# The tensor_tensor work of GpSimd moves to VectorE in a hybrid streaming-encoder block on one core

## The chip, the cores and the metric

The kernel runs on one core of a Trainium2 chip. Its time is the device time of one execution in microseconds (us). TensorE multiplies matrices into PSUM, VectorE and ScalarE work element by element on SBUF and PSUM, GpSimd does so on SBUF only, and SyncE issues the transfers between HBM and SBUF.

## The reference

One layer on a sequence of 2048 tokens with 1024 channels, all in float32. A token mixer and a channel mixer follow each other, each between two RMS norms, with a residual:

```
mix = token_mixer(rms_norm(x, pre_mix_g));       h = x + rms_norm(mix, post_mix_g)
ffn = channel_mixer(rms_norm(h, pre_ffn_g));     out = h + rms_norm(ffn, post_ffn_g)

token_mixer:   p = xn @ w_in
               group A: C * causal_conv3(B * hA)            512 channels
               group B: RWKV-7 mixing, 8 heads x 64, in chunks of 64 frames, then a group norm
               concat(A, B) @ w_out
channel_mixer: f = causal_conv3(hn @ w_up) + b              2 x 2816 channels
               (gelu(gate) * up) @ w_down
```

## The kernel before

Tensors lie channels by tokens, 128 channels on the partitions. The 2048 tokens are worked in four blocks of 512. Each float32 matrix product is made of three products of rounded halves: an operand is split into a high half (a ScalarE copy to the rounded type) and a low half (a subtraction, `split`, lines 484 to 486), and high x high, high x low and low x high are added in PSUM.

There are two plans, each with its own tiles. The first holds the token mixer: for each block the input projection (27 column groups of 128, eight weight tiles each, loaded four at a time by `gemm`, line 490), the RWKV mixing of two pairs of heads twice (features, scores, a triangular inverse by 31 steps of two VectorE instructions, a chain over eight chunks), the short convolution (`short_conv`, line 1148), then the output projection and the residual of the block ahead. The second plan holds the channel mixer: the up-projection of blocks 0 and 1 together (`up(0)`), two down-projections, the up-projection of blocks 2 and 3 (`up(1)`), two down-projections. The last output projection runs into `up(0)`, and two residuals are put beside its weight columns 8 and 14 (of 22).

What GpSimd does, apart from memsets at the start:

- In the first block `gemm` makes the low halves of the weights and keeps them in HBM; the later blocks load them from there. Low halves of the second four tiles of each column group (`keep and k0`) are made on GpSimd: 26 instructions.
- The first block's input norm is applied late, to products instead of the operand (`late` is its factor, broadcast). In `short_conv` two of these multiplies per column group are on GpSimd: 8 instructions.
- The up-projection multiplies two by two blocks of matrices with seven products instead of eight. The sums of weights that this wants are made in `up(0)` by `summed` (line 1342) and kept in HBM for `up(1)`. Of four sums per weight column, s1 (`wu0s`) and s3 (`wu2s`) are on GpSimd, s2 and s4 (both `wu1s`) on VectorE: 2 x 22 instructions on each.
- `finish` (line 1500) ends a down-projection: the norm's factor per token is spread over the partitions by a small product into PSUM (`over_partitions`, line 544; `fn_ps`), ScalarE copies it to SBUF (`fn_rb`), each of eight parts `fo` is multiplied by it and the residual `ho` is added, and the sum is stored. GpSimd multiplies parts 0 to 2 and adds parts 0 and 1, VectorE does the rest, reading the factor from PSUM. `ho` has two buffers, except in the last block, whose residuals are all held and whose tokens are finished in two halves of 256. `fo` lies in the eight buffers where the last operands of the next up-projection go.

The order on each engine is not that of the code. Every instruction is recorded with the instructions that it depends on, a rank and a modelled cost; `schedule` (line 364) lays them out as a list, the lowest rank first among those that are ready, `latest` (line 314) makes new ranks from how late each may start, and the best of 16 rounds is emitted. `cost` (line 264) gives a VectorE tensor_tensor of n columns 66 + 1.045 n ns and a GpSimd one 148 + 2.1 n ns: 601 and 1223 ns for 512 columns. Since all instructions are emitted at one place, the profile gives line 431 for nearly all; they are told apart by the tiles that they write and read.

Of the kernel before, what the change touches and what calls it, by code (L numbers as in the profile page):

```python
# [15 lines left out]
ALU = mybir.AluOpType  # L16
# [5 lines left out]
TB = 512  # L22
# [429 lines left out]
def tile_block(ctx: ExitStack, tc: tile.TileContext, x_tok, x_t, w_in, w_out, w_up, w_down,  # L452
# [3 lines left out]
    dve = nc.vector  # L456
    pool_e = nc.gpsimd
# [4 lines left out]
    o1 = plan.pool(ctx, "o1", 1)  # L462
# [27 lines left out]
    def gemm(ps, src, nk, xs, name, keep=None, early=False):  # L490

        old = plan.rank
        for k0 in range(0, nk, 4):
            n = min(4, nk - k0)
            plan.rank = R_PREP if early else R_WEIGHT
            raw = wst.tile([128, 4, 128], F32, tag="wraw", name=f"{name}_r{k0}", bufs=WB[0])
            nc.sync.dma_start(out=raw[:, 0:n, :], in_=src[:, k0:k0 + n, :])
            hi = wst.tile([128, 4, 128], F32R, tag="whi", name=f"{name}_h{k0}", bufs=WB[1])  # L500
            lo = wst.tile([128, 4, 128], F32R, tag="wlo", name=f"{name}_l{k0}", bufs=WB[1])
            if (keep, k0) in lower:
                act(hi, raw, AF.Copy)
                nc.sync.dma_start(out=lo.bitcast(F32), in_=lower[keep, k0])
            else:
                split(raw[:, 0:n, :], hi[:, 0:n, :], lo[:, 0:n, :],
                      pool_e if keep and k0 else dve)
                if keep:
                    lower[keep, k0] = dram.tile([128, 4, 128], F32, name=f"{keep}_l{k0}")
                    nc.sync.dma_start(out=lower[keep, k0], in_=lo.bitcast(F32))  # L510
            plan.rank = R_GEMM
            for k in range(n):
                wh, wl = hi[:, k, :], lo[:, k, :]
                ah, al = xs[k0 + k]
                nc.tensor.matmul(ps, wh, ah, start=(k0 + k == 0), stop=False)
                nc.tensor.matmul(ps, wh, al, start=False, stop=False)
                nc.tensor.matmul(ps, wl, ah, start=False, stop=(k0 + k == nk - 1))
        plan.rank = old
# [22 lines left out]
                          op0=ALU.mult, op1=ALU.add)  # L541
        rsqrt(o1, ms, [128, n], name, out=out)

    def over_partitions(y, name, pool, tag, bufs=1, both=False, n=4):

        dg = o1.tile([128, 4, 128], F32, tag="sq", name=f"{name}_dg")
        ps = psN.tile([128, TB], F32, tag="g", name=f"{name}_ps")
        for s in range(n):
            dve.tensor_scalar(out=dg[:, s, :], in0=ident, scalar1=y[:, s:s + 1], scalar2=None,
                              op0=ALU.mult)  # L550
        with plan.together():
            for s in range(n):
                nc.tensor.matmul(ps[:, s * 128:(s + 1) * 128], ones, dg[:, s, :],
                                 start=True, stop=True)
        rb = pool.tile([128, TB], F32, tag=tag, name=f"{name}_rb", bufs=bufs)[:, 0:n * 128]
        ps = ps[:, 0:n * 128]
        act(rb, ps, AF.Copy)
        return (rb, ps) if both else rb

    def token_sums(accs, name, n=4):  # L560

# [115 lines left out]
    with ExitStack() as mctx:  # L677
# [75 lines left out]
        with ExitStack() as ictx:  # L753
# [394 lines left out]
            def short_conv(b, j):  # L1148

                plan.rank = R_EVAC  # L1150
                nm = f"{b}_{j}"
                u = m1.tile([128, TB + 2], F32, tag="u", name=f"u{nm}", bufs=1)
                act(u[:, 0:2], ucar[:, j, :], AF.Copy)
                ps = proj(15 + 3 * j, f"ch{nm}")
                if late is None:
                    act(u[:, 2:TB + 2], ps, AF.Copy)
                else:
                    dve.tensor_tensor(out=u[:, 2:TB + 2], in0=ps, in1=late, op=ALU.mult)
                ps = proj(16 + 3 * j, f"cb{nm}")
                dve.tensor_tensor(out=u[:, 2:TB + 2], in0=ps, in1=u[:, 2:TB + 2], op=ALU.mult)  # L1160
                if late is not None:
                    pool_e.tensor_tensor(out=u[:, 2:TB + 2], in0=u[:, 2:TB + 2], in1=late,
                                         op=ALU.mult)
                act(ucar[:, j, :], u[:, TB:TB + 2], AF.Copy)
                cv = m1.tile([128, TB], F32, tag="cv", name=f"cv{nm}", bufs=1)
                act(cv, u[:, 2:TB + 2], AF.Copy, scale=v_("conv_a", 8 + j))
                dve.scalar_tensor_tensor(out=cv, in0=u[:, 1:TB + 1], scalar=v_("conv_a", 4 + j),
                                         in1=cv, op0=ALU.mult, op1=ALU.add)
                dve.scalar_tensor_tensor(out=cv, in0=u[:, 0:TB], scalar=v_("conv_a", j),
                                         in1=cv, op0=ALU.mult, op1=ALU.add)  # L1170
                ps = proj(17 + 3 * j, f"cc{nm}")
                dve.tensor_tensor(out=cv, in0=ps, in1=cv, op=ALU.mult)
                if late is not None:
                    pool_e.tensor_tensor(out=cv, in0=cv, in1=late, op=ALU.mult)
                nc.sync.dma_start(out=y_d[b][:, j, :], in_=cv)

            def first_operand():
# [111 lines left out]
    with ExitStack() as fctx:  # L1289
# [35 lines left out]
        def up_weights(s, i):  # L1325


            nm = f"{s}_{i}"

            def load(src, name, base=RAW, n=6):  # L1330
                raw = next_slot(base, n, f"wu{name}{nm}", F32, (128, 4, 128))
                nc.sync.dma_start(out=raw, in_=src)
                return raw

            def parts(raw, name):
                plan.rank = R_WEIGHT
                hi = wst.tile([128, 4, 128], F32R, tag="whi", name=f"wu{name}{nm}_h", bufs=WB[1])
                lo = wst.tile([128, 4, 128], F32R, tag="wlo", name=f"wu{name}{nm}_l", bufs=WB[1])
                split(raw, hi, lo, dve)
                return hi, lo  # L1340

            def summed(a, b, op, j, engine, o=None):
                plan.rank = R_WEIGHT
                if o is None:
                    o = next_slot(SUM, 2, f"wu{j}s{nm}", F32, (128, 4, 128))
                engine.tensor_tensor(out=o, in0=a, in1=b, op=op)
                nc.sync.dma_start(out=s_d[i][:, j, :, :], in_=o)
                return o

            plan.rank = R_WEIGHT  # L1350
            ga, gb, ua, ub = (w_up[j][:, k:k + 4, :] for j in (i, NF + i) for k in (0, 4))
            if s == 0:
                a11, a12, a21, a22 = (load(x, n) for x, n in ((ga, "a11"), (gb, "a12"),
                                                              (ua, "a21"), (ub, "a22")))
                yield parts(a11, "a11")
                s1 = summed(a21, a22, ALU.add, 0, pool_e)
                yield parts(s1, "s1")
                s2 = summed(s1, a11, ALU.subtract, 1, dve)
                yield parts(s2, "s2")
                yield parts(a12, "a12")  # L1360
                s3 = summed(a11, a21, ALU.subtract, 2, pool_e)
                yield parts(s3, "s3")
                s4 = summed(a12, s2, ALU.subtract, 3, dve, s2)
                yield parts(s4, "s4")
                yield parts(a22, "a22")
            else:
                for src, n in ((ga, "a11"), (s_d[i][:, 0, :, :], "s1"), (s_d[i][:, 1, :, :], "s2"),
                               (gb, "a12"), (s_d[i][:, 2, :, :], "s3"), (s_d[i][:, 3, :, :], "s4"),
                               (ub, "a22")):
                    plan.rank = R_WEIGHT  # L1370
                    yield parts(load(src, n, RAW, 8), n)
# [101 lines left out]
        def down_block(b, beside=None):  # L1473
# [26 lines left out]
            def finish(t, accs):  # L1500
# [3 lines left out]
                n = (t.stop - t.start) // 128  # L1504
                rf = f1.tile([128, 4], F32, tag="rf", name=f"rf{nm}")[:, 0:n]
                inv_rms(token_sums(accs, nm, n), nm, rf, n)
                rb, rps = over_partitions(rf, nm, o1, "nrb", both=True, n=n)
                for d in range(KT):
                    if last:
                        hk = held[d][:, t]  # L1510
                    else:
                        hk = f1.tile([128, TB], F32, tag="ho", name=f"ho{b}_{d}", bufs=2)
                        nc.sync.dma_start(out=hk, in_=h_d[b][:, d, :])
                    fd = fo[d][:, t]
                    if d < 3:
                        pool_e.tensor_tensor(out=fd, in0=fd, in1=rb, op=ALU.mult)
                    else:
                        dve.tensor_tensor(out=fd, in0=fd, in1=rps, op=ALU.mult)
                    (pool_e if d < 2 else dve).tensor_tensor(out=hk, in0=fd, in1=hk, op=ALU.add)
                    nc.sync.dma_start(out=out_t[:, b, d, t], in_=hk)  # L1520

            tokens = slice(0, TB)
# [123 lines left out]
```

## Time and profile before

| | |
|---|---|
| time, median of 3 runs | 2590.94 us (2590.84 to 2595.94) |
| profiled execution | 2591.45 us |
| its span, first to last instruction | 2589.7 us |
| TensorE busy | 2479.0 us (96%) |
| VectorE busy | 2025.0 us (78%), 4159 instructions |
| ScalarE busy | 1476.6 us (57%) |
| GpSimd busy | 152.8 us (6%), 116 instructions |
| mean granted TensorE clock | 0.986 of full speed |
| HBM traffic | 166 GB/s over the span |

Busy time is the time in which at least one instruction of the engine runs; two instructions that overlap count once. TensorE's share is an average over stages with different limits, so the stages are read one by one. The first block runs from 0 to about 260 us, the other blocks of the token mixer to about 1130, the first up-projection (with the two residuals) to about 1625, two down-projections to about 1890, the second up-projection to about 2320, and two down-projections to the end.

### The profile page before, as it was taken

To read this page: it belongs to the slowest core of one execution; us is meant where nothing else is said; L and a number is where in the kernel's file an instruction comes from. 1 tells how busy PE (TensorE), PEld (TensorE's weight loads), DVE (VectorE), ACT (ScalarE), POOL (GpSimd) and SP (SyncE) were. 2 spreads that over 40 slices of the span, in tenths; PEclk is the share of its full clock that TensorE was granted. 3 is DMA by queue.
4 is the path that set the end of the run, shared out by engine and by line. 5 is a ranking of instruction groups with operands and counts; after the bars stand their busy time and mean duration, and the time that the engine had idled before them with its cause. 6 is when DMAs were issued, how large, how long until landed. Compare 5 with 4: busy or idle time off the path is not lost.

```text
span 2589.7 us, 41292 instructions
## 1 busy us (share of the span) xinstructions
PE 2479.0 (96%) x14210; PEld 1948.8 (75%) x14210; DVE 2025.0 (78%) x4159; ACT 1476.6 (57%) x3070; POOL 152.8 (6%) x116
## 2 busy tenths in 40 slices
PE   8988999999999899989999999999989999999997
PEld 6766777777786677667877778788868888888886
DVE  7989878889786889768999999855478787784534
ACT  7555766566656555456656566543456666673532
POOL 1311000000000000001111121001010000000001
PEclk9999999999999899989999999999999999999998
DMA  6535454557454675465464634775654444454653
GB/s 204 175 100 167 130 172 131 165 163 257 130 171 148 203 248 163 150 202 179 154 192 147 202 131 167 249 247 172 190 183 126 122 118 130 120 160 130 191 183 106
DMA packets 239970, 432.29 MB, mean 167 GB/s; under 512 B 26640, under 2 KB 33424, under 8 KB 239760
## 3 DMA queue, kind: packets, MB, share of 16 engines
q1 hardware_dynamic: 239760, 429.65, 52.7%
q8 instruction: 112, 1.84, 0.3%
q14 instruction: 98, 0.80, 0.1%
HBM read 321.54 MB, written 108.00 MB: 166 GB/s over the span
## 4 chain that ended last, share of the span: by engine, by line
PE 64%; DVE 20%; DMA 8%; issue 4%; ACT 4%; SPq 0%; POOL 0%; DVEq 0%; ACTq 0%; POOLq 0%
PE dn L431 17%; PE upa L431 13%; PE upc L431 6%; PE op L431 5%; PE upb L431 3%; PE rp_ps L431 3%; PE kp_ps L431 2%; PE pc L431 2%; DVE cv L431 2%; PE vp_ps L431 2%; PE ch_ps L431 2%; PE cb_ps L431 1%; PE cc_ps L431 1%; DVE gt L431 1%; PE y L431 1%
## 5 line engine op out<-in xcount | busy, mean ns | idle before, releaser
L431 DVE TENSOR_TENSOR wd_l<-wd_r,wd_h 128x512 fp32r<-128x512 f32 x198 | 129.9, 658 | 200.0 <-ACT wd_h L431 190.9
L431 DVE SCALAR_TENSOR_TENSOR cv<-co,vec,cv 128x512 f32<-128x512 f32 x352 | 272.9, 800 | 13.5 <-ACT cv L431 12.1
L431 PE MATMUL dn<-gh,wd_h 128*128 128x512 f32 (+1 forms) x726 | 281.2, 388 | 0.9 <-ACT gh L431 0.6
L431 PE MATMUL dn<-gh,wd_l 128*128 128x512 f32 (+1 forms) x726 | 280.1, 386 | 0.2 <-DVE wd_l L431 0.2
L431 PE MATMUL dn<-gl,wd_h 128*128 128x512 f32 (+1 forms) x726 | 279.0, 384 | 0.2 <-DVE gl L431 0.2
L431 ACT ACTIVATE wd_h<-wd_r 128x512 fp32r<-128x512 f32 x198 | 117.4, 595 | 251.7 <-PE dn L431 220.4
L431 DVE SCALAR_TENSOR_TENSOR gt<-gt,cv 128x512 f32<-128x512 f32 x264 | 177.5, 694 | 2.0 <-ACT gt L431 0.8
L431 ACT ACTIVATE cv<-co,vec 128x512 f32<-128x512 f32 x176 | 142.3, 811 | 44.2 <-DVE co L431 35.4
L431 PEld LDWEIGHTS dn<-gl,wd_h 128*128 128x128 f32 x726 | 136.3, 188 | 30.2 <-DVE gl L431 1.3
L431 PEld LDWEIGHTS dn<-gh,wd_l 128*128 128x128 f32 x726 | 136.4, 188 | 30.0 <-DVE wd_l L431 0.4
L431 PEld LDWEIGHTS dn<-gh,wd_h 128*128 128x128 f32 x726 | 136.4, 188 | 29.3 <-ACT gh L431 1.7
L431 ACT ACTIVATE wua_h<-wua 128x512 fp32r<-128x512 f32 x132 | 82.6, 626 | 82.1 <-issue 38.4
L431 PE MATMUL op<-y_h,wo_h 128*128 128x512 f32 x256 | 101.6, 406 | 5.3 <-ACT y_h L431 4.2
L431 PE MATMUL op<-y_l,wo_h 128*128 128x512 f32 x256 | 102.4, 404 | 0.6 <-DVE y_l L431 0.4
L431 PE MATMUL op<-y_h,wo_l 128*128 128x512 f32 x256 | 101.7, 402 | 0.2
L431 DVE TENSOR_TENSOR wua_l<-wua,wua_h 128x512 fp32r<-128x512 f32 x132 | 96.9, 735 | 4.8 <-ACT wua_h L431 4.7
L431 ACT ACTIVATE wus_h<-wus 128x512 fp32r<-128x512 f32 x88 | 55.6, 632 | 68.2 <-PE upa L431 25.2
L431 DVE TENSOR_TENSOR ut<-nt,um 128x120 f32<-128x120 f32 (+24 forms) x248 | 70.0, 282 | 5.4
L431 DVE TENSOR_TENSOR um<-um,ut 128x120 f32<-128x120 f32 (+24 forms) x248 | 70.1, 283 | 5.2
L431 POOL TENSOR_TENSOR fo<-fo,fn_rb 128x512 f32<-128x512 f32 (+1 forms) x15 | 17.7, 1197 | 941.9 <-ACT fn_rb L431 941.9
L431 DVE TENSOR_TENSOR gl<-gk,gh 128x512 fp32r<-128x512 f32 x88 | 59.0, 687 | 16.1 <-ACT gh L431 15.9
L431 ACT ACTIVATE gt<-cv 128x512 f32<-128x512 f32 x88 | 55.0, 625 | 25.4 <-DVE cv L431 24.6
(731 smaller groups left out, 7081.0 us busy)
## 6 DMA issues: line engine op xcount, KB each, us to landing
wd_r<-in_w_down SPq DMA_DIRECT2D x165, 256.0 KB, 2.8
wua<-in_w_up SPq DMA_DIRECT2D x154, 256.0 KB, 3.0
g_d<-gt SPq DMA_DIRECT2D x88, 256.0 KB, 2.6
gk<-g_d SPq DMA_DIRECT2D x88, 256.0 KB, 3.3
wus<-s_d SPq DMA_DIRECT2D x88, 256.0 KB, 3.2
wo_r<-in_w_out SPq DMA_DIRECT2D x64, 256.0 KB, 3.3
s_d<-wu1s SPq DMA_DIRECT2D x44, 256.0 KB, 3.1
x<-in_x_t SPq DMA_DIRECT2D x32, 256.0 KB, 4.2
```

The source lines that it names most:

```text
L431: getattr(getattr(self.nc, e), m)(*[real(a) for a in args], **{k: real(a) for k, a in kw.items()})
```

## The change

Every tensor_tensor instruction of GpSimd is issued on VectorE instead; GpSimd keeps its memsets. In `finish` all eight parts read the norm's factor from PSUM, and the copy `fn_rb` of ScalarE is no longer made (`over_partitions` is called without a pool and returns the PSUM tile). The other callers of `over_partitions` get the copy as before. Planner, costs, ranks and tiles are otherwise the same, and the order is planned anew.

```diff
@@ gemm
-                split(raw[:, 0:n, :], hi[:, 0:n, :], lo[:, 0:n, :],
-                      pool_e if keep and k0 else dve)
+                split(raw[:, 0:n, :], hi[:, 0:n, :], lo[:, 0:n, :], dve)
@@ over_partitions
+        ps = ps[:, 0:n * 128]
+        if pool is None:
+            return ps
         rb = pool.tile([128, TB], F32, tag=tag, name=f"{name}_rb", bufs=bufs)[:, 0:n * 128]
-        ps = ps[:, 0:n * 128]
         act(rb, ps, AF.Copy)
-        return (rb, ps) if both else rb
+        return rb
@@ short_conv
-                    pool_e.tensor_tensor(out=u[:, 2:TB + 2], in0=u[:, 2:TB + 2], in1=late,
-                                         op=ALU.mult)
+                    dve.tensor_tensor(out=u[:, 2:TB + 2], in0=u[:, 2:TB + 2], in1=late,
+                                      op=ALU.mult)
...
-                    pool_e.tensor_tensor(out=cv, in0=cv, in1=late, op=ALU.mult)
+                    dve.tensor_tensor(out=cv, in0=cv, in1=late, op=ALU.mult)
@@ up_weights
-                engine.tensor_tensor(out=o, in0=a, in1=b, op=op)
+                dve.tensor_tensor(out=o, in0=a, in1=b, op=op)
...
-                s1 = summed(a21, a22, ALU.add, 0, pool_e)
+                s1 = summed(a21, a22, ALU.add, 0)
...
-                s3 = summed(a11, a21, ALU.subtract, 2, pool_e)
+                s3 = summed(a11, a21, ALU.subtract, 2)
@@ finish
-                rb, rps = over_partitions(rf, nm, o1, "nrb", both=True, n=n)
+                rps = over_partitions(rf, nm, None, "nrb", n=n)
...
-                    if d < 3:
-                        pool_e.tensor_tensor(out=fd, in0=fd, in1=rb, op=ALU.mult)
-                    else:
-                        dve.tensor_tensor(out=fd, in0=fd, in1=rps, op=ALU.mult)
-                    (pool_e if d < 2 else dve).tensor_tensor(out=hk, in0=fd, in1=hk, op=ALU.add)
+                    dve.tensor_tensor(out=fd, in0=fd, in1=rps, op=ALU.mult)
+                    dve.tensor_tensor(out=hk, in0=fd, in1=hk, op=ALU.add)
```

## Rows read from the trace of the kernel before

**Rows 1.** The page's first part: busy us (share of the span) and instructions by engine.
```profile
PE 2479.0 (96%) x14210; PEld 1948.8 (75%) x14210; DVE 2025.0 (78%) x4159; ACT 1476.6 (57%) x3070; POOL 152.8 (6%) x116
```
**Rows 2.** Busy time by stage: stretch, length, then busy us and instructions by engine.
```profile
0.00:260.00 260.00, 227.03 (x1464) 171.32 (x1465) 230.29 (x504) 154.51 (x343) 49.82 (x46) 0.97 0.50 162
260.00:1128.00 868.00, 838.51 (x6553) 632.71 (x6551) 702.58 (x1892) 522.04 (x1199) 0.00 (x0) 0.99 0.53 169
...
1178.00:1300.00 122.00, 120.90 (x532) 97.87 (x531) 111.79 (x174) 77.37 (x155) 19.50 (x13) 1.00 0.47 158
1300.00:1500.00 200.00, 190.40 (x817) 151.32 (x817) 193.04 (x310) 121.17 (x249) 29.85 (x18) 0.98 0.54 178
1500.00:1625.00 125.00, 121.27 (x524) 97.45 (x523) 119.28 (x181) 80.78 (x165) 21.52 (x12) 1.00 0.46 155
...
1885.00:1930.00 45.00, 33.01 (x127) 23.13 (x125) 36.71 (x63) 22.41 (x42) 8.09 (x5) 0.89 0.64 205
```
**Rows 3.** GpSimd's groups: count, busy us, mean ns of one, idle before and releaser.
```profile
L431 POOL TENSOR_TENSOR wu0s<-wua,wua 128x512 f32<-128x512 f32 x22 | 36.0, 1636 | 228.8 <-DVE wus_l L431 180.2 <-DMA wua<-in_w_up 14.6 <-DMA md<-mix_d 11.8
```
**Rows 4.** Timeline of VectorE and of GpSimd in the first up-projection: start us, us.
```profile
1276.19 0.68 DVE L431 TENSOR_TENSOR wus_l<-wu0s,wus_h 128x512 fp32r<-128x512 f32 x1
1276.79 3.11 DVE L431 SCALAR_TENSOR_TENSOR cv<-co,vec,cv 128x512 f32<-128x512 f32 x3
...
1280.43 0.74 DVE L431 SCALAR_TENSOR_TENSOR cv<-co,vec,cv 128x512 f32<-128x512 f32 x1
...
1276.96 1.73 POOL L431 TENSOR_TENSOR wu2s<-wua,wua 128x512 f32<-128x512 f32 x1 [6.18 <-DVE wus_l L431]
```
**Rows 5.** Timeline of VectorE and of GpSimd in the first block.
```profile
14.21 1.26 DVE L431 SCALAR_TENSOR_TENSOR x_l<-x,vec,x_h 128x512 fp32r<-128x512 f32 x1 [1.27 <-ACT x_h L431]
...
110.28 1.37 DVE L431 TENSOR_TENSOR ut<-nt,um 128x100 f32<-128x100 f32 x1
...
111.98 0.26 DVE L431 TENSOR_TENSOR ut<-nt,um 128x96 f32<-128x96 f32 x1
...
248.01 1.83 DVE L431 SCALAR_TENSOR_TENSOR x<-x,vec,pn_rb 128x512 f32<-128x512 f32 x1
...
110.24 1.29 POOL L431 TENSOR_TENSOR cc_l<-cc_r,cc_h 128x512 fp32r<-128x512 f32 x1 [4.83 <-DMA wi_l<-cb_l]
```
**Rows 6.** VectorE's groups in the stretch 1132 to 1620, the first up-projection.
```profile
L431 DVE SCALAR_TENSOR_TENSOR cv<-co,vec,cv 128x512 f32<-128x512 f32 x166 | 139.0, 859 | 4.1 <-ACT cv L431 3.4
...
L431 DVE TENSOR_TENSOR wua_l<-wua,wua_h 128x512 fp32r<-128x512 f32 x65 | 50.7, 780 | 1.9 <-ACT wua_h L431 1.9
...
L431 DVE TENSOR_TENSOR wu1s<-wu0s,wua 128x512 f32<-128x512 f32 x22 | 15.0, 682 | 3.8 <-POOL wu0s L431 3.8
```
**Rows 7.** VectorE's groups in the stretch 1925 to 2320, the second up-projection.
```profile
L431 DVE SCALAR_TENSOR_TENSOR cv<-co,vec,cv 128x512 f32<-128x512 f32 x162 | 116.4, 748 | 9.3 <-ACT cv L431 8.6
...
L431 DVE TENSOR_TENSOR wua_l<-wua,wua_h 128x512 fp32r<-128x512 f32 x60 | 41.0, 684 | 0.0
```
**Rows 8.** TensorE's waits, 1885 to 1930, then timelines of VectorE, GpSimd and SyncE.
```profile
PE upa L431 <- ACT t_13h L431: 3.4, 1, 3.4
PE upa L431 <- ACT t_12h L431: 3.4, 1, 3.4
...
1891.33 0.68 DVE L431 TENSOR_TENSOR fo<-fo,fn_ps 128x512 f32<-128x512 f32 x1
...
1895.76 3.43 POOL L431 TENSOR_TENSOR ho<-fo,ho 128x512 f32<-128x512 f32 x2
...
1903.67 0.87 SPq L431 DMA_DIRECT2D ho<-h_d  x2
```
**Rows 9.** Timeline of all engines from 2566 on, the finish of the last block's halves.
```profile
2571.56 1.42 DVE L431 TENSOR_TENSOR fo<-fo,fn_ps 128x256 f32<-128x256 f32 x4 [0.45 <-ACT fn_rb L431]
...
2581.27 0.42 DVE L431 TENSOR_TENSOR fo<-fo,fn_ps 128x256 f32<-128x256 f32 x1 [0.53 <-ACT fn_rb L431]
...
2584.63 1.63 DVE L431 TENSOR_TENSOR ho<-fo,ho 128x256 f32<-128x256 f32 x3
```

More of the change, by code (lines that the diff above doesn't have):

```diff
@@ L542, in inv_rms, with over_partitions @@
         rsqrt(o1, ms, [128, n], name, out=out)
-    def over_partitions(y, name, pool, tag, bufs=1, both=False, n=4):
+    def over_partitions(y, name, pool, tag, bufs=1, n=4):
         dg = o1.tile([128, 4, 128], F32, tag="sq", name=f"{name}_dg")
@@ L1340, in parts, with summed @@
                 return hi, lo
-            def summed(a, b, op, j, engine, o=None):
+            def summed(a, b, op, j, o=None):
                 plan.rank = R_WEIGHT
@@ L1355, in up_weights @@
                 yield parts(a11, "a11")
-                s1 = summed(a21, a22, ALU.add, 0, pool_e)
+                s1 = summed(a21, a22, ALU.add, 0)
                 yield parts(s1, "s1")
-                s2 = summed(s1, a11, ALU.subtract, 1, dve)
+                s2 = summed(s1, a11, ALU.subtract, 1)
                 yield parts(s2, "s2")
                 yield parts(a12, "a12")
-                s3 = summed(a11, a21, ALU.subtract, 2, pool_e)
+                s3 = summed(a11, a21, ALU.subtract, 2)
                 yield parts(s3, "s3")
-                s4 = summed(a12, s2, ALU.subtract, 3, dve, s2)
+                s4 = summed(a12, s2, ALU.subtract, 3, s2)
                 yield parts(s4, "s4")
```

## The prediction

> **What bounds the kernel now.** I read the busy times first, then the busy times by stage, then GpSimd's own groups, and last the timeline of VectorE beside GpSimd. TensorE is busy for 2479.0 of 2589.7 us and GpSimd for 152.8 [rows 1]: GpSimd is no bound, and the question is what its instructions do to others. By stage [rows 2] TensorE is not filled in four places: the first block (227.0 of 260.0), the stretch of the first up-projection that carries the residuals (190.4 of 200.0, VectorE 193.0), the stretch behind that (121.3 of 125.0, VectorE 119.3), and the turn from the second down-projection to the second up-projection (33.0 of 45.0 at a mean granted clock of 0.89). In 1300 to 1500 VectorE is the engine that sets the pace. In 1178 to 1300 TensorE does (120.9 of 122.0), so relief of VectorE is worth nothing there. The down-projections hold TensorE full; finishes that lie beside them cost nothing on either engine.
>
> One thing decides the sum. A sum of weights takes GpSimd 1.64 us in the mean [rows 3], but VectorE does not run freely meanwhile. In [rows 4] a lone cv takes 0.74 us; three in a row should take about 0.74 + 2 x 0.66 = 2.06 us (one instruction starts some 0.06 to 0.08 before the one ahead of it ends), and the three that start at 1276.79 take 3.11, just while GpSimd's sum runs from 1276.96 for 1.73. One VectorE instruction was held up for 1.05 us. The first block shows the same [rows 5]: a multiply of the inverse takes 0.26 us at 111.98 and, slightly larger, 1.37 us at 110.28, next to a GpSimd split that starts at 110.24 and takes 1.29. So a GpSimd instruction already costs VectorE time; the change swaps that hold-up for a VectorE instruction.
>
> The Trainium skill, "SBUF — State Buffer", section "Who interferes with whom", has a rule for it: a VectorE instruction with two inputs in SBUF and a GpSimd instruction share one read port, and whichever starts first holds it for its whole instruction. By that rule a hold-up could be as long as GpSimd's 1.64 us, 44 x 1.64 = 72 us for the weight sums. The trace shows the mechanism but a smaller size (1.05 and 1.1 us), and the sum goes by the trace.
>
> **The change, part by part.** 103 instructions move: 44 weight sums, 26 splits and 8 late norms in the first block, 25 in the four finishes. The price of one on VectorE is the distance of starts: 0.60 us for 128x512 (1276.19 to 1276.79 [rows 4]). The planner's formula has 601 ns for it already, and 1223 for GpSimd, against 1636 in the trace, and knows of no hold-up; nothing in the diff edits the formulas, so the new order comes from numbers that fit better than the old order's did.
>
> *Weight sums.* Added: 44 x 0.60 = 26.4 us of VectorE. Given back: cv takes 859 ns here [rows 6] against 748 in the second up-projection, where GpSimd is idle [rows 7], 166 x 0.111 = 18.4 us; the split of the loaded weights 780 against 684, 65 x 0.096 = 6.2 us. With nothing else that is 24.6 us, the lower end; 28 us by one pattern repeated (1.05 us beside the second sum, 0.2 beside the first, 22 times). If every sum held VectorE for 1.05 us it would be 46, the upper end. I take 30, nearest to the pattern plus smaller groups (the residual's instructions, small roots). VectorE also waited 3.8 us for wu0s [rows 6], which goes: 0.68 us on its own queue replaces 1.64. Net for VectorE: 26.4 - 30 - 3.8 = -7.4 us, bounds +1.8 (24.6 back and no wait saved) to -23. Only where VectorE sets the pace does it count: of 447 us from 1178 to 1625, 325 us lie in such stretches, 0.73 x 7.4 = 5.4. I take -5 us, bounds +2 to -13 (TensorE's idle time in 1300 to 1625: 9.6 + 3.7). What is late next is the DMA of the residual and ScalarE's copies out of PSUM.
>
> *First block.* Added: 26 splits and 8 late multiplies, 34 x 0.60 = 20.4 us. Given back: 24 VectorE instructions (the first at 14.21, the last at 248.01 [rows 5]) take 0.5 to 1.1 us more than their form does alone, together about 22 us. Net -2 us of VectorE, which is busy 230 of 260 us; nine of the held ones are steps of the triangular inverse, a chain that nothing else replaces. A late norm also becomes 0.9 us shorter, and a split 0.7. Against it, a split now stands in VectorE's queue and waits there for its ScalarE half, with scores and inverse behind it; the planner places it, but by modelled DMA times. I take -2 us, bounds -12 and +12 (a bit over a third of TensorE's 33 idle us, either way).
>
> *Finishes and the turn.* For blocks 0 and 2, 15 - 5 = 10 instructions lie beside a full TensorE: nothing. Block 1's finish lies on the path: TensorE waits 3.4 us for t_12h and 3.4 for t_13h [rows 8], which lie in the buffers fo that this finish frees. The products are in PSUM at 1891.3, where VectorE's first multiply starts; GpSimd starts its adds at 1895.76 and ends them 3.43 later at 1899.2; only then do stores, and at 1903.67 the loads of the next two parts, follow [rows 8], and so on round the two buffers of ho. On VectorE two multiplies and two adds take 2.4 us. Could they run at once, the adds would end at 1893.7, 5.5 us earlier; splits queue there too, and 5 x 0.60 = 3.0 us is added against some 4 us of hold-ups given back. I take -4 us, bounds 0 (the loads set the pace whatever starts them) to -8 (with part of the 5 us lost to the lower clock, 45 x 0.11).
>
> *The tail.* In the last half block VectorE idles 0.53 us for ScalarE's copy fn_rb, which is gone, then takes from 2581.27 to 2586.26 for its 4 multiplies and 6 adds [rows 9], held up beside GpSimd. Afterwards 16 instructions of 128x256 stand there; their distance is (1.42 - 0.42) / 3 = 0.33 us in the run of four [rows 9], 16 x 0.33 + 0.08 = 5.4 us from 2580.3 (nothing waits for the copy): 2585.7. That is -0.5 us, bounds -2 and +2 (the middle half's root may be queued behind all of its 16).
>
> Sum: -5 - 2 - 4 - 0.5 = -11.5 us. The profiled execution took 2591.45 us for a span of 2589.7; 2591.45 - 11.5 = 2580. The median of the runs, 2590.94, is 0.5 lower, less than I can tell apart.
>
> *What lies outside the sum.* Both programs are re-planned as a whole, so stretches with no edited instruction get another order. The nearest row is 260 to 1128, where TensorE idles 29.5 of 868 us [rows 2]; a third of it either way, 10 us, is the price that I give that.
>
> *A rule that speaks against it.* The Trainium skill, "VectorE: DVE Perf Modes", section "The DRAIN you can't avoid", has the next VectorE instruction start only when the pipe is empty, and its advice is to minimise the count. The trace shows starts 0.60 apart for a duration of 0.68 [rows 4], and the sum goes by that; what the rule would make of it is a rival below.
>
> **The rivals.**
>
> *An even swap.* Hold-ups come back at the lower end (24.6 us), the turn goes at the pace of its loads, and the first block gains nothing: +1.8 x 0.73 = +1.3, 0, 0, -0.5: about 2592. For it: TensorE is 96% busy, and a bound of that kind ignores the rest. Against it: VectorE's 193 of 200 us where the residuals run.
>
> *Every moved instruction costs its whole duration and a wait.* Sums feed the next instruction of the same engine, so they may not overlap: 0.68 + 0.1 us. Then the sums cost 44 x 0.78 = 34.3 (net +0.5 after 30 and 3.8 us) and the first block 34 x 0.78 = 26.5 (net +4.5); with -4 and -0.5 it is 2592. The rule of the Trainium skill on the pipe, above, points there. Against it: the distances that the rows show.
>
> *The queue of the first block (slower).* GpSimd's waits for ScalarE's halves were free; in VectorE's queue they are not. The price: each of 34 instructions delays the chain by 0.60 us, 20.4, and only the nine hold-ups on the inverse (9 x 1.03 = 9.3) were on the chain, so +11; if the order of later blocks suffers by a third as much as it could, +10 more; with -5, -4 and -0.5 this gives 2603. It decides once the first block grows by more than the 9.5 us that the rest gives. For it: VectorE sets that block's chain; against it: held time elsewhere there was VectorE's queue too.
>
> **How the numbers follow.** Forecast 0.58, even swap 0.18, whole durations 0.08, queue 0.16. A measurement of this kernel tells about 0.2% (5.2 us) from no change, so the forecast's 2580 counts as faster, the swap and whole durations as the same, the queue as slower. The likeliest case alone holds 2572 to 2586. The range is 2567 to 2597: below, the up-projection's and the turn's better ends (-13, -8, -3); above, the swaps and the weaker half of the queue case.
>
> **What would show it.** Right: GpSimd has memsets only; cv in the first up-projection takes about 0.75 us instead of 0.86; VectorE's busy time over the span changes by under 15 us although it has 103 instructions more; TensorE is fuller than 190.4 in the 200 us with the residuals; the adds of block 1's finish start within 3 us of its first multiply, and the wait for t_13h shrinks. Wrong: if cv stays above 0.8 us with GpSimd idle, the hold-ups were not GpSimd's; if the first block is longer than 265 us, the queue case holds; if 260 to 1128 moves by more than 10 us, the order decided.

## The result and the profile after

The changed kernel takes 2560.87 us (median of 4 runs, 2555.32 to 2562.8) against 2593.44 for the kernel before on the same chip (2590.84 to 2597.02): a ratio of 0.987, 95% interval 0.9847 to 0.9892. The sign is as forecast; the time lies 6 us below the predicted range. Between the two profiled executions the span falls by 28.9 us, from 2589.7 to 2560.8.

The first part of the page answers to [rows 1]:

```profile
PE 2471.7 (97%) x14210; PEld 1957.0 (76%) x14210; DVE 2012.9 (79%) x4262; ACT 1476.9 (58%) x3065; POOL 2.2 (0%) x13
```

VectorE has 103 instructions more and is busy for 12.1 us less. TensorE has the same 14210 matmuls and is busy for 7.3 us less.

To see where the time went, both programs were cut at the same pieces of work. A tile's view gives, after the mean lengths, when its first and its last matmul starts; here the first product of the first up-projection (upa with t_00h) and the first of the down-projections (dn). Before:

```profile
L431 PE MATMUL upa<-t_00h,wus_h x44: 388/394/505, 1185.2 to 1622.3; 128*128 128x512 f32 x44
...
L431 PE MATMUL dn<-gh,wd_h x726: 274/394/501, 1630.3 to 2571.8; 128*128 128x512 f32 x171, 128*128 128x256 f32 x11
```

After:

```profile
L431 PE MATMUL upa<-t_00h,wus_h x44: 388/394/505, 1186.7 to 1604.0; 128*128 128x512 f32 x44
...
L431 PE MATMUL dn<-gh,wd_h x726: 276/394/503, 1609.8 to 2545.0; 128*128 128x512 f32 x171, 128*128 128x256 f32 x11
```

With the same cut at the second up-projection (upa with t_10h), the pair of profiles gives:

| stretch | before, us | after, us | difference |
|---|---|---|---|
| token mixer, up to the first upa | 1185.2 | 1186.7 | +1.5 |
| up(0), first upa to first dn | 445.1 | 423.1 | -22.0 |
| two down-projections, to the first upa of up(1) | 256.7 | 255.1 | -1.6 |
| up(1), first to last upa of t_10 | 428.3 | 425.3 | -3.0 |
| two down-projections, to the last dn | 256.5 | 254.8 | -1.7 |
| behind the last dn | 17.9 | 15.8 | -2.1 |

Three quarters of the gain are in one stretch. Busy times in up(0), columns as in [rows 2], first before and then after:

```profile
1185.20:1630.30 445.10, 430.67 (x1860) 345.07 (x1859) 422.03 (x652) 278.85 (x568) 69.59 (x42) 0.99 0.50 165
```

```profile
1186.70:1609.80 423.10, 421.52 (x1854) 344.35 (x1854) 411.59 (x693) 282.87 (x566) 0.00 (x0) 1.00 0.52 172
```

Now TensorE is busy for 421.5 of 423.1 us: it sets the pace of the whole stretch, and VectorE follows with 11.5 us idle. Of the 22 us that went, 12.8 were idle time of TensorE (14.4 to 1.6) and 9.2 were counted as busy, for practically the same matmuls (some records are missing in either).

What those 9.2 us are can be read from the starts of TensorE's matmuls. Where it is fed, a matmul of 512 columns starts 0.23 us after the one ahead of it, while its record lasts 0.39 us; so at each stop some 0.16 us of waiting counts as busy. Before has 20 stops in this stretch, after has 5: an estimate of 2.5 us. And before, the granted clock falls twice for 3.4 us to its lower level (0.50, 1.2 of 2.4 GHz), at 1340.6 and at 1453.2, both times shortly behind a wait of TensorE (2.91 and 3.35 us). After, it does not fall in this stretch. Around the second fall, before:

```profile
1447.85 0.39 PE L431 MATMUL upc<-t_00h,wus_l 128*128 128x512 f32 x1
1448.08 0.39 PE L431 MATMUL upc<-t_01h,wus_h 128*128 128x512 f32 x1
1451.82 0.51 PE L431 MATMUL upa<-t_00h,wus_h 128*128 128x512 f32 x1 [3.35 <-ACT m L431]
...
1453.48 0.63 PE L431 MATMUL upc<-t_02h,wus_h 128*128 128x512 f32 x1
1453.90 0.63 PE L431 MATMUL upc<-t_02l,wus_h 128*128 128x512 f32 x1
```

```profile
1453.20:1456.60 3.40, 3.40 (x10) 2.62 (x9) 2.33 (x5) 2.19 (x7) 0.00 (x0) 0.50 0.79 208
```

At the lower clock matmuls of 512 columns start 0.43 us apart, and the dozen of them in the two falls cost some 2.4 us more. The rest of the 9.2 is pauses too short to show as idle, and six records more.

VectorE's groups from 1132 to 1605 answer to [rows 6]:

```profile
L431 DVE SCALAR_TENSOR_TENSOR cv<-co,vec,cv 128x512 f32<-128x512 f32 x166 | 120.7, 746 | 1.6 <-ACT cv L431 1.4
...
L431 DVE TENSOR_TENSOR wua_l<-wua,wua_h 128x512 fp32r<-128x512 f32 x65 | 44.5, 685 | 0.0
...
L431 DVE TENSOR_TENSOR wu0s<-wua,wua 128x512 f32<-128x512 f32 x22 | 15.1, 688 | 0.2
L431 DVE TENSOR_TENSOR wu1s<-wu0s,wua 128x512 f32<-128x512 f32 x22 | 15.1, 688 | 0.1
```

And the stretches of [rows 2] from 1178 to 1625:

```profile
1178.00:1300.00 122.00, 122.00 (x542) 100.30 (x542) 113.84 (x192) 79.25 (x158) 0.00 (x0) 1.00 0.48 160
1300.00:1500.00 200.00, 198.42 (x877) 161.42 (x876) 196.37 (x344) 130.45 (x262) 0.00 (x0) 1.00 0.56 185
1500.00:1625.00 125.00, 125.00 (x551) 102.52 (x550) 124.51 (x202) 90.61 (x180) 0.00 (x0) 1.00 0.55 177
```

These windows reach further into the work than before, since it is earlier; still TensorE is full in all three, also where the residuals run (198.4 of 200, before 190.4). VectorE is as full as it was: it is no longer late. In the groups above, cv takes 746 ns, as in the second up-projection, and nothing waits for wu0s any more. The timeline of VectorE at the place of [rows 4]:

```profile
1276.49 0.69 DVE L431 TENSOR_TENSOR wu2s<-wua,wua 128x512 f32<-128x512 f32 x1
1277.10 1.41 DVE L431 SCALAR_TENSOR_TENSOR cv<-co,vec,cv 128x512 f32<-128x512 f32 x2
...
1279.03 2.07 DVE L431 SCALAR_TENSOR_TENSOR cv<-co,vec,cv 128x512 f32<-128x512 f32 x3
```

In the first line the sum starts 0.61 us ahead of the next instruction, the price that the prediction gave it, and three cv in a row take 2.07 us where they took 3.11.

### The profile page after: what moved, and what is told of

Its sections match the earlier page's. It is cut to its first block, busy times and chain, and to the rows that moved or that the text cites. A ratio compares the mean times of both kernels' runs of the same rounds, so it can differ in the third digit from the quotient of the medians.

```text
span 2560.8 us, 41170 instructions
## 1 busy us (share of the span) xinstructions
PE 2471.7 (97%) x14210; PEld 1957.0 (76%) x14210; DVE 2012.9 (79%) x4262; ACT 1476.9 (58%) x3065; POOL 2.2 (0%) x13
## 4 chain that ended last, share of the span: by engine, by line
PE 75%; DVE 12%; DMA 8%; ACT 3%; issue 2%; SPq 0%; DVEq 0%; ACTq 0%
PE dn L431 18%; PE upa L431 17%; PE upc L431 8%; PE op L431 5%; PE upb L431 4%; PE pc L431 2%; PE kp_ps L431 2%; PE vp_ps L431 2%; PE rp_ps L431 2%; PE ch_ps L431 2%; PE cb_ps L431 2%; PE cc_ps L431 2%; DMA x<-in_x_t 1%; PE y L431 1%; DMA xt<-in_x_tok 1%
## 5 line engine op out<-in xcount | busy, mean ns | idle before, releaser
L431 DVE SCALAR_TENSOR_TENSOR cv<-co,vec,cv 128x512 f32<-128x512 f32 x352 | 254.3, 747 | 11.0 <-ACT cv L431 10.1
L431 DVE TENSOR_TENSOR wua_l<-wua,wua_h 128x512 fp32r<-128x512 f32 x132 | 90.4, 685 | 3.1 <-ACT wua_h L431 2.6
L431 ACT ACTIVATE gh<-gk 128x512 fp32r<-128x512 f32 x88 | 55.0, 627 | 28.8 <-DMA gk<-g_d 26.0
L431 ACT ACTIVATE sv<-sn,pct 64x64 f32<-64x64 f32 x112 | 32.5, 336 | 66.1 <-DVE sn L431 65.6
L431 DVE TENSOR_TENSOR gl<-gk,gh 128x512 fp32r<-128x512 f32 x88 | 59.4, 688 | 12.3 <-ACT gh L431 11.8
L431 DVE TENSOR_TENSOR ut<-nt,um 128x120 f32<-128x120 f32 (+24 forms) x248 | 64.8, 261 | 5.0 <-ACT um L431 0.3
```

The costliest lines, as they stand in the source:

```text
L431: getattr(getattr(self.nc, e), m)(*[real(a) for a in args], **{k: real(a) for k, a in kw.items()})
```

## The experiments

In all of them TensorE's matmuls are those of the kernel before. A single profile of a program scatters by some us in the token mixer (below), so a stage is read from its own marks; `up(0)` is the stretch of the table above. Four experiments at a time (e1 to e4, e5 to e8 and so on) share a chip, and the kernel before is timed beside them on it; programs on different chips are compared by their ratios.

### Which part of the change: e1 and e2

e1 does the weight sums alone, e2 all the rest.

```diff
 e1, in the kernel before
-                s1 = summed(a21, a22, ALU.add, 0, pool_e)
+                s1 = summed(a21, a22, ALU.add, 0, dve)
-                s3 = summed(a11, a21, ALU.subtract, 2, pool_e)
+                s3 = summed(a11, a21, ALU.subtract, 2, dve)
 e2, in the kernel after: the same two lines back on pool_e
```

> Only the 44 weight sums go to VectorE, all else as before, planned anew; the first plan keeps the order of before. Theory A (the sums alone): the first up-projection was 445 us before and 424 after, so the kernel is 18 to 24 us faster than before, some 2571, with TensorE full (over 0.99) in that stretch. Theory B (the gain needs the other moves as well): less than 12 us faster.

> All moves but the weight sums. Theory A: 4 to 9 us faster than before (the turn and the ends of the finishes; the token mixer ended 2 us later in the changed kernel and does so here). Theory B: over 12 us faster.

e1: 2574.62 us against 2597.12, ratio 0.9913 (0.9898 to 0.9928). e2: 2584.25, ratio 0.9947 (0.9931 to 0.9963). That is -22.5 and -12.9 us; their sum of -35.4 stands beside -32.6 for the whole change, so the parts add up. up(0) takes 422.9 us in e1 and 446.3 in e2: the sums alone make the stretch short, and nothing else of the change touches it. The 12.9 us of e2 are outside the 4 to 9 of theory A and over the 12 named for B. The stretch still speaks for A; what had been put too low is the rest, above all the first block, where a single profile had shown no gain (e10 and e11 below).

### Hold-ups or the plan: e3 and e4

Two things change with the sums: VectorE is not held up any more, and the planner now has the sum as 601 ns on VectorE, with a place in VectorE's list, instead of 1223 ns on GpSimd. A recorder was added that plans an instruction for one engine and issues it on another. In e3 the order is the old one and VectorE does the sums; in e4 the order is that of e1, and GpSimd does them. The traces bear this out: without the sums, VectorE's and ScalarE's instructions come in the same sequence in e3 as before, and in e4 as in e1.

```diff
-                e = ops[i][0]
+                e = self.real.get(i, ops[i][0])
...
 e3: planned for GpSimd, issued on VectorE; e4 the other way round
+    moved = _Recorder(plan, "gpsimd", "vector")
-                s1 = summed(a21, a22, ALU.add, 0, pool_e)
+                s1 = summed(a21, a22, ALU.add, 0, moved)
 (s3 alike)
```

> The 44 weight sums are planned as GpSimd instructions at GpSimd's modelled cost, so every engine has the order of before, but they are issued on VectorE at the place that their planned start gives. Theory H (a GpSimd instruction holds VectorE, and that is the whole cost): 15 to 24 us faster than before, with the order of before. Theory O (the order planned anew is what gains): within 5 us of before.

> The 44 weight sums are planned as VectorE instructions, so the order is that of the kernel with only the sums moved, but they are issued on GpSimd. Theory H: the hold-ups are back, cv at 0.83 us or more, and the time is within 6 us of before. Theory O: 12 to 20 us faster than before although GpSimd works.

e3: 2581.09 us, ratio 0.9931 (0.9914 to 0.9947). e4: 2585.70, ratio 0.9953 (0.9938 to 0.9968). Both are faster than before, by about half each. Busy times in up(0), e3, then e4, then e1:

```profile
1192.80:1623.90 431.10, 425.61 (x1861) 344.92 (x1860) 416.92 (x695) 280.57 (x569) 0.00 (x0) 1.00 0.52 170
```

```profile
1189.20:1622.50 433.30, 425.15 (x1846) 341.59 (x1845) 417.40 (x646) 278.10 (x562) 70.81 (x42) 1.00 0.51 167
```

```profile
1189.40:1612.30 422.90, 420.92 (x1845) 343.23 (x1844) 410.23 (x686) 280.29 (x564) 0.00 (x0) 1.00 0.51 170
```

And cv in VectorE's groups of the stretch, e3, then e4:

```profile
L432 DVE SCALAR_TENSOR_TENSOR cv<-co,vec,cv 128x512 f32<-128x512 f32 x162 | 117.8, 745 | 3.1 <-ACT cv L432 2.6
```

```profile
L432 DVE SCALAR_TENSOR_TENSOR cv<-co,vec,cv 128x512 f32<-128x512 f32 x162 | 132.8, 842 | 3.2 <-ACT cv L432 3.0
```

In e3 the hold-ups are gone and the order is old: -14.0 us. In e4 the hold-ups are there (842 ns, GpSimd busy for 70.8 us) and the order is new: -11.8 us. Together they would make -25.8; e1 has -22.2, and TensorE is full there (420.9 of 422.9). The 16.0 us of e3 are what theory H asked for; the 11.4 of e4 lie between the 6 of H and the 12 of O, so neither theory holds alone. In e3 a sum also takes 0.69 us instead of 1.64 and comes without a wait for GpSimd; e3 does not tell this from the hold-ups, and e5 below looks at the hold-ups by themselves.

From e4 to e1, with one order on all other engines, VectorE's busy time falls by 7.2 us although it takes over the 42 sums that lie in the stretch, at 42 x 0.60 = 25.2; so the sums held it up for 32.4 us. From before to e3, in the old order, it falls by 5.1, which makes 30.3. The prediction had 30. That part of it was right, and the effect of the order was not in its sum at all.

### What GpSimd does to VectorE: e5 and e6

Beside each of the 44 sums, the changed kernel gets GpSimd work into a scratch tile that nobody reads, issued without being planned, so that the order stays. In e5 it is two tensor_tensor of 192 columns of the sum's operands, in e6 one of 8 columns and then seven memsets.

```diff
+                if j in (0, 2):
+                    plan.extra[len(plan.ops)] = [tt(c, 192) for c in (0, 192)]
 e6 instead:
+                    plan.extra[len(plan.ops)] = [tt(0, 8)] + [("memset", (beside, 0.0), {})] * 7
```

> The changed kernel, its order kept; beside each of the 44 moved sums GpSimd also adds the same two operands, 2 x 192 columns, into a small buffer that nobody reads. No work is moved back, only GpSimd's reads of SBUF return. Theory H (hold-ups of VectorE make the stage longer): cv goes from 746 to over 790 ns and the first up-projection from 423 to 433 to 450 us, the kernel 10 to 27 us slower than the changed one. Theory O (the order alone counts, hold-ups fit into VectorE's idle time): under 5 us.

> As the last, but beside each moved sum GpSimd reads only 8 columns and then fills a small buffer with zeros seven times, about as long as a sum took it. If only GpSimd's reads hold VectorE: cv stays under 760 ns and the kernel within 4 us of the changed one. If any access of GpSimd to SBUF holds it: as the last kernel, 10 us slower or more.

e5: 2574.21 us, ratio 0.9919 (0.9896 to 0.9942), 13 us slower than the changed kernel. e6: 2561.78, ratio 0.9862 (0.9838 to 0.9886), the same as the changed kernel. Busy times in up(0), e5, then e6:

```profile
1180.00:1618.10 438.10, 427.24 (x1853) 342.43 (x1852) 428.92 (x700) 281.38 (x565) 96.52 (x84) 1.00 0.50 167
```

```profile
1179.70:1605.40 425.70, 422.90 (x1854) 343.80 (x1853) 412.34 (x700) 282.23 (x566) 107.72 (x336) 1.00 0.52 172
```

And what GpSimd does in e6:

```profile
L435 POOL MEMSET beside<- 128x192 f32 x294 | 76.2, 259 | 17.0
L435 POOL TENSOR_TENSOR beside<-wua,wua 128x8 f32<-128x8 f32 x42 | 31.5, 750 | 331.5 <-DMA wua<-in_w_up 329.8
```

GpSimd is busy for longer in e6, yet only e5 holds VectorE up: 428.9 against 411.6 us busy, +17.3, and the stretch grows by 15.0; in e6 they grow by 0.7 and 2.6. So what GpSimd reads is the cost, not that it runs. It is not that VectorE's operands came later in e5: it idles for 9.2 us there, not more than the 11.5 of the changed kernel. One expectation for e5 was missed: cv rises to 771 ns and not over 790; other groups rise too (the split wua_l from 685 to 724 ns, the sum wu0s from 688 to 799). The Trainium skill, "SBUF — State Buffer", section "Who interferes with whom", has a VectorE instruction with two SBUF inputs contend with a GpSimd instruction that reads SBUF and not with one that only writes it; the trace agrees (cv 771 ns in e5, 744 in e6). The two numbers also price VectorE in this stretch: 0.87 us of the stretch for each us of it.

### Luck of the order: e7, e8 and e12

A plan can come out better by chance. e7 gives the planner a GpSimd sum of 1633 ns, as traced, e8 and e12 another constant of the planner, in the kernel before and in the one after.

```diff
 e7
-        base, each = {"tensor_tensor": (148, 2.1), "tensor_scalar": (430, 0.63),
+        base, each = {"tensor_tensor": (148, 2.9), "tensor_scalar": (430, 0.63),
 e8, e12
-STAY = 10.0
+STAY = 14.0
```

> The kernel before; only the planner's number for a GpSimd tensor_tensor is changed, from 2.1 to 2.9 ns per column (1223 to 1633 ns for 512, the measured mean). Theory O1 (the old order was poor because GpSimd took longer than planned): the first up-projection falls from 445 to 436 us or less, near the 433 of the new order on GpSimd. Rival O2 (what the plan lacks is the hold-up of VectorE, which this does not tell it): 441 us or more.

> The kernel before; only the planner's weight against changes of kind on TensorE is changed, 10 to 14, which gives another order of the whole and tells the planner nothing new. Rival L (a new order moves the time by luck): over 6 us either way, or the first up-projection changes by over 6 us. Otherwise within 5 us of before and the stage within 4.

> The changed kernel with the planner's weight against changes of kind on TensorE at 14 for 10: another order of everything that tells the planner nothing new. If the stage is at TensorE's own time whatever the order: the first up-projection stays at 421 to 426 us, and the kernel within 8 us of the changed one, either way. If 423 was a lucky order: over 430 us.

e7: 2602.08 us, ratio 1.0021 (1.0009 to 1.0034), up(0) 445.3. e8: 2590.45, ratio 0.9983 (0.997 to 0.9996), up(0) 444.7. e12: 2561.66, ratio 0.9868 (0.9851 to 0.9884), up(0) 422.4. Three other orders with the sums on GpSimd (e2, e7, e8) give 444.7 to 446.3, another with them on VectorE 422.4: no luck. In all runs, the stretch takes 442.5 to 456.4 us where the sums are GpSimd's in the plan and in fact (before, e2, e7 to e11, e13), and 422.4 to 423.1 where they are VectorE's in both (after, e1, e12). Nor was it that GpSimd's sum is planned too short: with its traced duration the stretch stays at 445.

### What in the new plan helps: e9, e14 and e13

The theory that was left: the plan has to keep VectorE's time for a sum free, whoever executes it, since a sum on GpSimd takes that time from VectorE too. e9 and e14 plan a VectorE tensor_tensor beside each GpSimd sum and never issue it. In e9 it writes a tile that nobody reads; in e14 it writes the sum's own tile ahead of the sum, so the sum and all that follows must wait for it in the plan.

```diff
+                if e == "none":
+                    continue
...
+    unissued = _Recorder(plan, "vector", "none")
...
 e9
+                    held = f1.tile([128, 4, 128], F32, tag="held", name=f"held{j}{nm}")
+                    unissued.tensor_tensor(out=held, in0=a, in1=b, op=op)
 e14
+                    unissued.tensor_tensor(out=o, in0=a, in1=b, op=op)
 e13, in the kernel before
-        base, each = {"tensor_tensor": (148, 2.1), "tensor_scalar": (430, 0.63),
+        base, each = {"tensor_tensor": (148, 0.885), "tensor_scalar": (430, 0.63),
```

> The kernel before, the sums on GpSimd at their old modelled cost, but the plan also sees a VectorE tensor_tensor of 601 ns with the same operands beside each of them, which is never issued. Theory O2 (the old order was poor because the plan did not know that a GpSimd sum takes time from VectorE): the first up-projection falls from 445 to 437 us or less. Rival O3 (the order on GpSimd gained because the sums were placed as short instructions of VectorE's own queue): 441 us or more.

> The kernel before; the plan sees a VectorE tensor_tensor of 601 ns ahead of each GpSimd sum, writing the same buffer, so it lies in the chain of that sum and cannot be put off; it is never issued. Theory O2: the first up-projection at 437 us or less, though GpSimd holds VectorE as before. Theory O4: 441 us or more.

> The kernel before; the planner counts 601 ns for a GpSimd tensor_tensor of 512 columns (0.885 for 2.1 ns per column), on GpSimd's own queue. Theory O4 (a sum planned as short places its splits and loads better): the first up-projection at 437 us or less. Theory O2 (the plan must know that the sum takes time from VectorE): 441 us or more.

e9: 2592.18 us, ratio 0.9992 (0.9983 to 1.0002), up(0) 442.5: nothing. Since nothing depends on the tile, the planner can put the instruction off, and so it does: in the plan that e9's kernel file makes, it starts 5 to 38 us behind its sum from the eighth weight column on, for 30 of the 44. So this was no fair test of the theory. e14 closes that way out: 2581.69 us, ratio 0.9943 (0.9924 to 0.9963). Its up(0), and its cv:

```profile
1188.90:1623.70 434.80, 427.30 (x1870) 344.41 (x1868) 420.19 (x659) 276.92 (x565) 78.21 (x42) 1.00 0.52 170
```

```profile
L434 DVE SCALAR_TENSOR_TENSOR cv<-co,vec,cv 128x512 f32<-128x512 f32 x161 | 134.5, 859 | 1.6 <-ACT cv L434 1.4
```

The instructions on all engines are those of the kernel before, GpSimd does the sums, cv is held up to the same 859 ns, and the stretch is 10.3 us shorter. What does it is the time that the plan keeps free on VectorE in the sum's chain. That the chain is longer in this plan (601 ns and 1223 behind it) does not do it alone: e7 planned the sum at 1633 ns and gained nothing. e13 plans the GpSimd sum at 601 ns, VectorE's value, and is slower: 2609.12 us, ratio 1.0057 (1.0038 to 1.0077), up(0) 456.4. So it is not the shorter planned duration either; short and with no place on VectorE makes the plan worse. Which instructions the better plans place otherwise, and which wait that saves, was not traced.

### The two halves once more: e15 and e16

e3 and e4, with the planner's constant of e8.

```diff
 e3 and e4, with
-STAY = 10.0
+STAY = 14.0
```

> The sums planned for GpSimd and issued on VectorE, once more, with the planner's weight at 14 for 10, so that the order is another one. If the gain is that of the hold-ups: the first up-projection at 427 to 436 us. If 431 was luck: 440 us or more.

> The sums planned for VectorE and issued on GpSimd, once more, with the planner's weight at 14 for 10. If the gain is that of the plan's knowledge: the first up-projection at 429 to 438 us. If 433 was luck: 441 us or more.

e15: 2581.31 us, ratio 0.9944 (0.9921 to 0.9967), up(0) 432.7, 12.0 below e8. e16: 2583.92, ratio 0.9947 (0.9927 to 0.9966), up(0) 436.0, 8.7 below e8. Both halves are there in a second pair of plans.

### The first block: e10 and e11

Its 26 splits and 8 late norms move alone: in e10 in the old order, in e11 planned anew.

```diff
 e10 (in e11 dve instead of moved)
+    moved = _Recorder(plan, "gpsimd", "vector")
-                      pool_e if keep and k0 else dve)
+                      moved if keep and k0 else dve)
-                    pool_e.tensor_tensor(out=cv, in0=cv, in1=late, op=ALU.mult)
+                    moved.tensor_tensor(out=cv, in0=cv, in1=late, op=ALU.mult)
 (the late norm of u alike)
```

> Only the first block's 26 splits and 8 late multiplies are issued on VectorE, in the order that was planned for GpSimd; sums and finishes stay on GpSimd. Theory H (hold-ups): the last sum of the output projection, at 1187 us in the median of four profiles with the old first plan, falls by 3 to 9 us. Rival L (the 8 us that the first plan gained came by another order): within 2 us, or later.

> The same moves, planned anew. The first plan is then that of the changed kernel: last sum of the output projection near 1179, the first up-projection as before at 445 us, and the kernel 4 to 10 us faster than before. By theory H this is the gain of the last kernel and a little more, by L all of it is the order.

e10: 2588.58 us, ratio 0.9978 (0.9967 to 0.9989), -5.5 us. e11: 2585.03, ratio 0.9965 (0.9951 to 0.998), -9.1 us. The larger part, as far as the intervals tell, comes with the old order, so it is the move itself. Whether that is the hold-ups or the shorter splits and late norms was not separated: no run brings GpSimd's reads alone back into the first block. In e10's profile the last sum lies at 1177.7 us, 9.6 below the median of 1187.3 given next, a little more than the 3 to 9 that were expected. Single profiles can't say much finer: the six that share the kernel before's first plan and issue it as it does (before, e1, e3, e4, e9, e14) end the token mixer (the last matmul of on_tsum) at 1183.4 to 1190.9 us, median 1187.3, the five that share the changed kernel's (after, e2, e5, e6, e11) at 1178.6 to 1185.8, median 1179.1. With the planner's constant at 14 the gain is hardly seen: 1180.2, 1185.3 and 1185.5 with the first block's work on GpSimd (e8, e16, e15), 1183.0 with it on VectorE (e12). So the first block's gain is shown for one pair of plans. The profile of the changed kernel is the latest of those five, which is why the first line of the table above shows no gain, and why the two spans lie 28.9 us apart and the medians of the runs 32.6.

## Why the prediction was right in sign and wrong in size

*The mechanism* stands: GpSimd's instructions hold VectorE up for longer than VectorE needs to do them itself (30.3 to 32.4 us against 25.2 for 42 sums), 0.60 us is the price of one on VectorE, and VectorE's busy time over the span changes by -12.1 us with 103 instructions more, inside the 15 that was asked for.

*The step that failed is the size of the weight sums*: "Only where VectorE sets the pace does it count: of 447 us from 1178 to 1625, 325 us lie in such stretches, 0.73 x 7.4 = 5.4. I take -5 us, bounds +2 to -13". It was -22.0, of which the move alone gives -14.0 in the old order (e3) and the plan alone -8.7 to -11.8 (e16, e4). Of the 21 us between the -11.5 forecast in all and the -32.6 measured, 17 lie in this term. Three things were wrong in it:

- The bound. It was TensorE's idle time, 13.3 us in 1300 to 1625. But before, TensorE's busy time contained 9.2 us that were gone with the waits, short pauses and the lower clock behind long ones: the same matmuls take 430.7 us before and 421.5 after, at a granted clock of 0.99 and 1.00. The true floor was the 421 us that TensorE needs when it is fed, and it lay 24 us below the 445.1.
- The plan. The prediction said that the new order "comes from numbers that fit better than the old order's did" and then gave this no term here; its ±10 us for new orders was put on the token mixer. It is worth 8.7 to 11.8 us in this stretch (e4, e14, e16).
- The net for VectorE. Its busy time fell by 10.4 us and its idle time by 11.6 (23.1 to 11.5), where -7.4 in all was reckoned. The hold-ups of 30 to 32 us were near the 30 taken. What was missed is idle time, and not all of it is the plan's: in the old order (e3) it already falls by 8.9 us, of which the wait for wu0s is 3.8; the waits for the residual's loads (md) fall there from 4.2 to 0.9, and the sum had no term for such waits.

*The first block* was put at -2 us and gave -5.5 to -9.1 (e10, e11), within the bounds of ±12. TensorE is busy there for 234.9 of 260 us, before 227.0 [rows 2]:

```profile
0.00:260.00 260.00, 234.90 (x1487) 179.31 (x1488) 226.59 (x541) 158.15 (x350) 2.06 (x12) 0.96 0.52 165
```

37 more instructions take 3.7 us less of VectorE: for 34 x 0.60 = 20.4 us added, some 24 came back, a little over the estimated 22. The prediction set this off one for one, and the block gained more than the difference; that it came back on the chain fits this, but was not shown. The queue of the first block, the rival on the slower side, does not show.

*The finishes and the turn* were put at -4 us. up(1) takes 424.6 to 427.5 us in the five profiles with the finish on VectorE and 428.3 to 432.3 in the other twelve and the kernel before; the means, 425.9 and 430.0, lie 4.1 apart. The path is the one described: the timeline of VectorE and of SyncE answers to [rows 8],

```profile
1869.06 1.28 DVE L431 TENSOR_TENSOR fo<-fo,fn_ps 128x512 f32<-128x512 f32 x2
1870.25 1.29 DVE L431 TENSOR_TENSOR ho<-fo,ho 128x512 f32<-128x512 f32 x2
...
1873.73 0.91 SPq L431 DMA_DIRECT2D ho<-h_d  x2
```

the adds end 2.5 us after the first multiply starts, before 7.9, and the loads of the next parts go out 4.7 us after it instead of 12.3. One sign was wrong: the wait for t_13h did not shrink. TensorE's waits in the turn after are

```profile
PE upa L431 <- ACT t_13h L431: 5.0, 1, 5.0
PE upa L431 <- DVE t_12l L431: 1.6, 1, 1.6
```

instead of 3.4 for each of t_12h and t_13h; all its waits in the 45 us of the turn make 10.2 us against 11.7. The last operand still comes last. The gain does lie in the turn: in the 45 us behind the first upa of up(1) TensorE starts a dozen matmuls more, at 0.23 us each 2.8 of the 3.0 us of this pair. Before, then after:

```profile
1887.00:1932.00 45.00, 33.01 (x126) 23.04 (x125) 35.51 (x56) 21.81 (x40) 8.09 (x5) 0.89 0.63 201
```

```profile
1864.90:1909.90 45.00, 34.67 (x138) 25.60 (x137) 36.81 (x63) 22.75 (x42) 0.00 (x0) 0.89 0.63 205
```

*The tail* was put at -0.5 us and gave -2.2 (16.0 us against 18.1 behind the last dn, means over the profiles with either finish). The prediction priced VectorE's run in the last half alone. The timeline before, then after:

```profile
2570.69 0.42 DVE L431 TENSOR_TENSOR fo<-fo,fn_ps 128x256 f32<-128x256 f32 x1 [0.70 <-PE fn_ps L431]
...
2576.23 0.15 DVE L431 TENSOR_SCALAR fn_ms<-fn_tsum 128x2 f32<-128x2 f32 x1
```

```profile
2543.78 2.74 DVE L431 TENSOR_TENSOR fo<-fo,fn_ps 128x256 f32<-128x256 f32 x8
...
2547.77 0.16 DVE L431 TENSOR_SCALAR fn_ms<-fn_tsum 128x2 f32<-128x2 f32 x1
```

The half ahead has eight multiplies in 2.74 us, and the root of the last half starts 4.0 us after the first of them; before it was 5.5 us, from 2570.69 to 2576.23. That root was the price that the prediction named as a danger, and it came earlier.

*Outside the sum* nothing moved by the 10 us that were kept for it: in 260 to 1128 TensorE is busy for 833.1 us against 838.5, and no profile of a program with the new first plan ends the token mixer that much later. All three rivals fall: no even swap (the interval ends at 0.9892), no whole durations (the sum at 1276.49 starts 0.61 us ahead of the next instruction and lasts 0.69), no queue.

## What to carry to other kernels

An instruction that goes to an engine which takes its operands from the same place as a busy engine is not free; price it by what it adds to its neighbours' durations, and if a program plans the order, let it book that time on the neighbour, in the chain of the work that needs the result (booked where it could be put off, in e9, it did nothing). TensorE's idle time is no bound on what a starved stretch can gain: compare its busy time with that of the same matmuls in a stretch where it is fed. When a change both moves work and plans anew, issue the new engine in the old order, and the old engine in the new order: the two halves can be as large as each other.

## What the runs showed of the hardware that was not expected

- A GpSimd tensor_tensor of 128x512 costs VectorE 0.72 to 0.77 us in the mean (30.3 and 32.4 us for 42), more than the 0.60 us that VectorE takes to do it itself. GpSimd's own sums take 1.64 to 1.66 us before and 1.81 to 1.90 in e14; why was not shown, for VectorE is as full in e4, where they take 1.65 to 1.73.
- GpSimd's writes cost VectorE next to nothing: 76.2 us of memsets in e6 leave cv at 744 ns and VectorE's busy time in the stretch within 0.7 us.
- TensorE's busy time can shrink by 9.2 us of 430.7 with the same matmuls, when what feeds it comes sooner: short pauses count as busy, and behind two waits of about 3 us the granted clock was 0.50 for 3.4 us each.
